# A float32 transpose of 8192 x 8192: store rows of 8 KB instead of 4 KB, pieces parked in shared slots and gathered by VectorE

## The chip, the cores and the metric

The kernel runs on one core of a Trainium2 chip. The metric is the device time of one launch in microseconds (us), as the median of several runs. Beside the runs there is one profiled execution, whose span goes from its first to its last instruction. Engines are called by their names or as the profile has them: PE (TensorE, its weight loads PEld), ACT (ScalarE), DVE (VectorE), POOL (GpSimd), SP (SyncE). Transfers between HBM and the on-chip memory (SBUF) run on 16 DMA engines, which take them from queues; the queue of ScalarE is q10 in the profile, that of SyncE q1.

## The reference

```python
def setup_inputs():
    return {"x": np.random.randn(8192, 8192).astype(np.float32)}

def reference(x):
    return np.transpose(x)
```

There is no arithmetic: 268 MB are read and 268 MB are written, with rows and columns exchanged.

## The kernel before

**Tiles.** The input is cut into chunks of 128 rows by 4096 columns, 2 MB each. Two bands of 4096 columns with 64 chunks each make 128 chunks, numbered t. A chunk is loaded into one of three input buffers (`ins`, `NIN = 3`), 16 KB in each of the 128 partitions. A *range* is a group of neighbouring columns of a band, which become rows of the output. Before the change a range has 512 columns (`B = 4` columns in each partition), and a band has 8 ranges.

**A chunk's way.** TensorE transposes the chunk with an identity matrix in 32 blocks of 128 x 128 (L117) into two PSUM tensors, one for each half of the ranges. It counts `s_pe` up as it goes. ScalarE copies the first half to SBUF and VectorE the second (both L241). A chunk gives each range one *piece*.

**Windows and stores.** The pieces of one range from 8 consecutive chunks (`W = 8`) lie side by side in one of 9 store buffers (`regs`, `NREG = 9`). Together they are a *window*: 2 MB, 16 KB in each partition, that is 4 output rows of 8 x 128 elements, 4 KB each. `wide_dma` (L28) describes a store so that the 16 KB of a partition are one packet with 4 rows at its far end. The ranges are staggered, so that exactly one window closes with each chunk. At the start, at the end, and where the second band begins, windows are shorter or come in two parts.

**The order.** Nothing is planned by a framework; the instructions are written out, and semaphores order them. The first three loads are issued by SyncE, all other loads (L103) and all stores (L28, the first L174) by ScalarE between its copies. In the steady part (`later(t)`) a store of a window that closed in chunk t is issued once the first transposes of chunk t+1 are done (`nc.scalar.wait_ge(s_pe, (t + 1) * NH + 1)`), and behind it the load of chunk t+3. TensorE starts a chunk when its load has landed and both copying engines are done with the chunk before (18 counts on `s_ld`). A copy that opens a window waits until the store that used its buffer has landed (`fresh`).

Of the kernel before, what the change touches and what calls it, by code (L numbers as in the profile page):

```python
# [40 lines left out]
def kernel(  # L41
# [22 lines left out]
    NR = S // B  # L64
    NIN = 3
    NREG = 9
    CH = N // P
    J = S * P

    with tc.tile_critical():  # L70
        nc.alloc_sbuf_tensor("pad", [P, 32], dt)
        ident = nc.alloc_sbuf_tensor("ident", [P, P], dt).ap()
        ins = [nc.alloc_sbuf_tensor(f"in{k}", [P, J], dt).ap() for k in range(NIN)]
        SIZE = B * W * P
        regs = nc.alloc_sbuf_tensor("regs", [P, NREG * SIZE], dt).ap()
        NH = NR // 2
        pss = [nc.alloc_psum_tensor(f"ps{k}", [P, NH * B * P], dt).ap() for k in range(2)]
# [3 lines left out]
        s_st = [nc.alloc_semaphore(f"s_st{k}") for k in range(NREG)]  # L81
        s_pe = nc.alloc_semaphore("s_pe")
        s_cp = [nc.alloc_semaphore("s_cpa"), nc.alloc_semaphore("s_cpv")]

# [3 lines left out]
            out=ident,  # L88
            in_=ident,
# [6 lines left out]
        nc.vector.sem_inc(s_ld[0], 1)  # L96
        nc.scalar.sem_inc(s_ld[0], 1)

        chunks = [(s, c) for s in range(M // J) for c in range(CH)]

        def load(t):
            s, c = chunks[t]
            (nc.sync if t < NIN else nc.scalar).dma_start(  # L103
                out=ins[t % NIN], in_=x[c * P:(c + 1) * P, s * J:(s + 1) * J]
            ).then_inc(s_ld[t % NIN], 16)

        def transposes(k):
            nc.tensor.sem_inc(s_ld[k], -18).wait_op(s_ld[k], 18, "sem-ge")  # L113
            for q in range(NR):
                e, g = divmod(q, NH)
                for b in range(B):
                    tr = nc.tensor.transpose(  # L117
                        pss[e][:, (g * B + b) * P:(g * B + b + 1) * P],
                        ins[k][:, q * B * P + b:(q + 1) * B * P - B + b + 1:B],
                        ident,  # L120
                    )
                if q % 2:
                    tr.then_inc(s_pe, 1)

        T = len(chunks)
        assert T % NIN == NIN - 1
        pe = [nc.tensor.engine]
        nc.tensor.wait_ge(s_id, 2)

# [13 lines left out]
        for t in range(NIN):  # L143
            load(t)

        copied = [0, 0]
        free = list(range(NREG))
        stored = [0] * NREG
        window = {}

        def later(t):
            return W <= t < T - NIN

        def store(q, e, t):
            t0, r, parts = window.pop(q)
            if later(t):
                nc.scalar.wait_ge(s_pe, (t + 1) * NH + 1)
            else:
                nc.scalar.wait_ge(s_cp[e], copied[e])
            base = 0  # L160
            pieces = []
            for s, a, z in parts:
                rows = (z - a) * P
                j0 = s * J + q * B * P
                dst = out[j0:j0 + B * P, a * P:a * P + rows]
                dst = dst.rearrange("(q b) i -> q b i", q=P)
                src = regs[:, r * SIZE + base:r * SIZE + base + B * rows]
                base += B * rows
                pieces.append((rows, dst, src))
            for rows, dst, src in sorted(pieces, key=lambda v: -v[0]):  # L170
                if any(stored):
                    st = wide_dma(nc, nc.scalar, "qActDynamicHW", dst, src)
                else:
                    st = nc.scalar.dma_start(  # L174
                        out=dst, in_=src.rearrange("q (b i) -> q b i", b=B)
                    )
                st.then_inc(s_st[r], 16)
                stored[r] += 1
            free.append(r)

        def closes(w, t):
            t0, r, parts = w
            return t + 1 == t0 + sum(z - a for _, a, z in parts)

        for t, (s, c) in enumerate(chunks):
            closed = []
            for e in range(2):
                eng = (nc.scalar, nc.vector)[e]
                go = s_ld[(t + 1) % NIN]

                place = []
                fresh = {}
                for q in range(e * NH, (e + 1) * NH):
                    if q not in window:

                        span = (q - c) % W + 1
                        r = free.pop(0)
                        parts = [(s, c, min(c + span, CH))]  # L200
                        if c + span > CH and t + span < T:
                            parts.append((s + 1, 0, c + span - CH))
                        window[q] = (t, r, parts)
                        if stored[r]:
                            fresh[q - e * NH] = (s_st[r], 16 * stored[r])
                    t0, r, parts = window[q]
                    k = [p[0] for p in parts].index(s)
                    base = r * SIZE + B * P * sum(z - a for _, a, z in parts[:k])
                    _, a, z = parts[k]
                    place.append((base + (c - a) * P, (z - a) * P))  # L210

                runs = []
                for g in range(NH):
                    if runs:
                        u = runs[-1]
                        gap = place[g][0] - place[g - 1][0]
                        if place[g][1] == place[u[0]][1] and abs(gap) < 2 ** 15 and (
                            len(u) == 1 or gap == place[u[1]][0] - place[u[0]][0]
                        ):
                            u.append(g)  # L220
                            continue
                    runs.append([g])
                if later(t):
                    runs = sorted(runs, key=lambda u: any(g in fresh for g in u))
                seen = t * NH + e * NH // 2
                for u in runs:
                    off, dist = place[u[0]]
                    gap = place[u[-1]][0] - place[u[-2]][0] if len(u) > 1 else 0
                    dims = [list(regs.ap[0]), [gap, len(u)], [dist, B], [1, P]]
                    o = bass.AP(regs.tensor, regs.offset + off, dims)  # L230
                    i = pss[e][:, u[0] * B * P:(u[-1] + 1) * B * P]
                    i = i.rearrange("p (l b i) -> p l b i", b=B, i=P)
                    need = t * NH + (e * NH + u[-1]) // 2 + 1
                    if later(t) and u is runs[0] and len(runs) > 1 and any(g in fresh for g in runs[-1]):
                        need = t * NH + (e * NH + max(v[-1] for v in runs)) // 2 + 1
                    if need > seen:
                        eng.wait_ge(s_pe, need)
                        seen = need
                    for sem, value in [fresh[g] for g in u if g in fresh]:
                        eng.wait_ge(sem, value)  # L240
                    cp = nc.scalar.copy(out=o, in_=i) if e == 0 else nc.vector.tensor_copy(out=o, in_=i)  # L241
                    ends = [e * NH + g for g in u if closes(window[e * NH + g], t)]
                    if later(t):
                        if u is runs[-1]:
                            cp.then_inc(go, 1)
                        closed += [(q, e) for q in ends]
                        continue
                    if ends:
                        cp.then_inc(s_cp[e], 1)
                        copied[e] += 1  # L250
                    if u is runs[-1]:
                        if ends:
                            eng.wait_ge(s_cp[e], copied[e])
                            eng.sem_inc(go, 1)
                        else:
                            cp.then_inc(go, 1)
                    for q in ends:
                        store(q, e, t)
            for q, e in closed:
                store(q, e, t)  # L260
            if t + NIN < T:
                if not closed:
                    nc.scalar.wait_ge(s_pe, (t + 1) * NH)
                load(t + NIN)
        for r in range(NREG):
            nc.sync.wait_ge(s_st[r], 16 * stored[r])
# [30 lines left out]
```

## Time and profile before

| what | us |
|---|---|
| median of 3 runs | 1262.53 (1261.64 to 1262.58) |
| span of the profiled execution | 1260.4 |
| VectorE busy in it | 302.0 |
| ScalarE busy in it | 253.5 |
| TensorE busy in it | 739.0 |

The page gives no other time for the profiled execution than its span; it is 2.1 us below the median of the runs, which also hold what lies around the first and the last instruction.

How to read the lines shown below. In a group of instructions stand line, engine, operation, output and input with their shapes, the count, then the busy time and the mean ns of one, then the idle time of the engine ahead of them and what ended it. In a timeline each line has start, duration, engine, line and operation, and in brackets the idle time before it; ACTq and SPq are DMA issues by ScalarE and SyncE. In windows each line is a stretch of the span with its length, then the busy time of each engine with its instructions (x), and last the granted clock of TensorE, the DMA share (busy share of the 16 engines, which can read 1.01 where packets overlap) and GB/s. In DMA issues the last number is the median time from the issue to the landing. Busy shares are averages over the span; what bounds a stretch is read from that stretch.

### The profile page before, as it was taken

How to read it: one execution, taken by the hardware profiler on the slowest of the kernel's cores; microseconds unless marked ns; L12 is line 12 of the kernel's file. 1: busy time of each engine (PE TensorE's matmuls, PEld its weight loads, DVE VectorE, ACT ScalarE, POOL GpSimd, SP SyncE). 2: the span in 40 equal slices, each digit the busy share in tenths (PEclk: the TensorE clock that was granted, in tenths of full speed). 3: DMA queues.
4: the chain of work that ended last, by engine and by line, in shares of the span. 5: the costliest groups of instructions: out<-in, count | busy, mean ns of one | idle time of the engine just before them, and what ended most of it. 6: DMA issues, size and time to landing. Idle time of an engine off the chain costs nothing. (4 is left out here: it accounts for less than half of the span.)

```text
span 1260.4 us, 9367 instructions
## 1 busy us (share of the span) xinstructions
PE 739.0 (59%) x4096; PEld 718.4 (57%) x4096; DVE 302.0 (24%) x250; ACT 253.5 (20%) x257; POOL 0.7 (0%) x6
## 2 busy tenths in 40 slices
PE   5656556565566655565556656566565655665561
PEld 5556556565556655565555656565565655665561
DVE  2322222222222222222222222222222222222220
ACT  3212211122111211122111211121111211121110
POOL 0000000000000000000000000000000000000000
PEclk9886876868777777778687786867777687777776
DMA  9999999999999999999999999999999999999998
GB/s 383 429 422 426 425 430 431 426 431 431 427 430 431 428 428 431 428 429 432 427 422 426 429 429 425 431 429 428 430 428 428 431 428 429 429 429 429 429 431 376
DMA packets 39271, 536.95 MB, mean 426 GB/s; under 512 B 4320, under 2 KB 4832, under 8 KB 6240
## 3 DMA queue, kind: packets, MB, share of 16 engines
q10 hardware_dynamic: 38832, 530.60, 99.0%
q1 hardware_dynamic: 432, 6.29, 1.2%
q14 instruction: 6, 0.05, 0.0%
q8 instruction: 1, 0.02, 0.0%
HBM read 268.44 MB, written 268.44 MB: 426 GB/s over the span
## 5 line engine op out<-in xcount | busy, mean ns | idle before, releaser
L117 PE MATMUL ps<-ident,in 128*128 128x128 f32 x4096 | 739.0, 362 | 493.5 <-PEq L113 493.5
L117 PEld LDWEIGHTS ps<-ident,in 128*128 128x128 f32 x4096 | 718.4, 220 | 513.9 <-issue 513.9
L241 DVE COPY regs<-ps 128x512 f32<-128x512 f32 (+3 forms) x250 | 302.0, 1246 | 932.1 <-PE ps L117 932.1
L241 ACT COPY regs<-ps 128x512 f32<-128x512 f32 (+3 forms) x256 | 252.2, 1016 | 978.8 <-PE ps L117 760.8
L241 ACT ACT_TABLE_LOAD x1 | 1.3, 1283 | 1.0 <-SPq L70 1.0
L87 POOL TENSOR_SCALAR_AFFINE_SELECT ident<-ident 128x128 f32<-128x128 f32 x1 | 0.3, 293 | 0.2 <-POOL ident L85 0.2
L85 POOL MEMSET ident<- 128x128 f32 x1 | 0.2, 204 | 0.5 <-SPq L70 0.5
L281 POOL MEMSET const-bfloat16-1.0<- 128x1 bf16 x1 | 0.1, 102 | 0.0
L281 POOL MEMSET const-uint8-127<- 128x1 uint8 x1 | 0.1, 102 | 0.0
L281 POOL MEMSET const-float32-0.0<- 128x1 f32 x1 | 0.1, 99 | 0.2 <-issue 0.2
L281 POOL MEMSET const-float32-1.0<- 128x1 f32 x1 | 0.1, 99 | 0.0
## 6 DMA issues: line engine op xcount, KB each, us to landing
in<-in_x_dram ACTq DMA_DIRECT2D x125, 2048.0 KB, 16.8
out_dram<-regs ACTq DMA_DIRECT2D x114, 2048.0 KB, 12.6
out_dram<-regs ACTq DMA_DIRECT2D x4, 1792.0 KB, 11.1
in<-in_x_dram SPq DMA_DIRECT2D x3, 2048.0 KB, 11.7
out_dram<-regs ACTq DMA_DIRECT2D x4, 1536.0 KB, 12.5
out_dram<-regs ACTq DMA_DIRECT2D x4, 1280.0 KB, 11.5
out_dram<-regs ACTq DMA_DIRECT2D x4, 1024.0 KB, 11.1
out_dram<-regs ACTq DMA_DIRECT2D x4, 768.0 KB, 12.3
```

What stands on the lines that cost most here:

```text
L85: nc.gpsimd.memset(ident, 0.0).then_inc(s_id, 1)
L87: nc.gpsimd.affine_select(out=ident, in_=ident, compare_op=mybir.AluOpType.not_equal, fill=1.0, base=0, pattern=[[-1, P]], channel_multipl ...
L117: tr = nc.tensor.transpose(pss[e][:, (g * B + b) * P:(g * B + b + 1) * P], ins[k][:, q * B * P + b:(q + 1) * B * P - B + b + 1:B], ident,)
L241: cp = nc.scalar.copy(out=o, in_=i) if e == 0 else nc.vector.tensor_copy(out=o, in_=i)
L281: nc = _bacc.Bacc("TRN2", target_bir_lowering=False, num_devices=1)
```

## The change

A range now has 256 columns (`B = 2`), so a band has 16 ranges (`NR = 16`), and a window collects 16 chunks. A full window is still 2 MB with 16 KB in each partition, now as 2 output rows of 8 KB.

Sixteen open windows of 2 MB don't fit in SBUF. So a piece isn't put where it will be stored from. It waits in a *slot*. The slot of range r and chunk t is found from the pair of r and m = t mod 16, and the pair (r, m) shares its slot with (m, r): 120 slots of 128 KB each. Window w (range w mod 16) closes with chunk w. Before the copies of chunk w VectorE gathers the window's earlier pieces, up to 15, from their slots into a place in the `arena` (`gather`), and counts `s_g` up. The last piece is copied from PSUM straight to that place by ScalarE or VectorE, ahead of the other pieces of its quarter, and counts `s_cl` up. Both engines' copies of chunk t wait for `s_g` to reach t, since they write into slots which that gather empties.

The arena holds the three input buffers and 38 pieces more. A loop at build time gives each window a place in it (`home`) and notes whose store must have landed before (`before`); near the end the places may lie in input buffers, and the gather then waits for the transposes of the buffer's last chunk.

TensorE waits for each half of PSUM by itself (`s_free`) and signals after each quarter of a chunk instead of each pair of ranges. All loads and stores are issued by SyncE: `store(t)` waits for `s_cl`, and behind it come the loads. Up to chunk 15 and from chunk 124 on, loads are issued up to chunk t+3, between them up to t+2. After the last chunk 15 short windows are gathered and stored. The gathers of windows 127 and 128 are begun a chunk early, ahead of the copies of chunks 126 and 127.

```diff
-    S = 32
-    B = 4
-    W = 8
+    B = 2
+    NR = 16
+    W = NR
+    J = NR * B * P
     NIN = 3
-    NREG = 9
+    PIECE = B * P
+    FIN = 38
+    NQ = 4
+    QR = NR // NQ
...
+        slots = nc.alloc_sbuf_tensor("slots", [P, (NR * (NR - 1) // 2) * PIECE], dt).ap()
+        arena = nc.alloc_sbuf_tensor("arena", [P, NIN * J + FIN * PIECE], dt).ap()
...
         def transposes(k):
-            nc.tensor.sem_inc(s_ld[k], -18).wait_op(s_ld[k], 18, "sem-ge")
+            for h in range(2):
+                nc.tensor.sem_inc(s_free[h], -1).wait_op(s_free[h], 1, "sem-ge")
+                if h == 0:
+                    nc.tensor.sem_inc(s_ld[k], -16).wait_op(s_ld[k], 16, "sem-ge")
...
+                    if g % QR == QR - 1:
+                        tr.then_inc(s_pe, 1)
...
+        def slot(r, t):
+            m = t % W
+            d = (r - m) % W
+            if d < W // 2:
+                return ((d - 1) * W + m) * PIECE
+            if d > W // 2:
+                return ((W - d - 1) * W + r) * PIECE
+            return ((d - 1) * W + min(r, m)) * PIECE
...
+        def gather(w, upto):
+            from_ = begun.get(w, max(0, w - W + 1))
+            begun[w] = upto
+            for u in before.pop(w, []):
+                if isinstance(u, tuple):
+                    nc.vector.wait_ge(s_pe, (u[1] + 1) * NQ)
+                else:
+                    nc.vector.wait_ge(s_st[u % W], done[u])
...
+            if r < NR // 2 and runs:
+                nc.vector.wait_ge(s_cp[0], upto)
+            for v in runs:
+                so, do, dist = v[0]
+                ss, ds = (v[1][0] - so, v[1][1] - do) if len(v) > 1 else (PIECE, P)
+                cp = nc.vector.tensor_copy(
+                    out=ap(arena, do, [[ds, len(v)], [dist, B], [1, P]]),
+                    in_=ap(slots, so, [[ss, len(v)], [P, B], [1, P]]),
+                )
+            if runs and upto == min(w, T):
+                cp.then_inc(s_g, 1)
...
+        def copies(t):
+            for e, eng in enumerate((nc.scalar, nc.vector)):
+                if t:
+                    eng.wait_ge(s_g, t)
+                for h in range(NQ // 2):
+                    eng.wait_ge(s_pe, t * NQ + e * NQ // 2 + h + 1)
...
+                    runs.sort(key=lambda v: (v[0][1] is not None))
...
+        def store(w):
+            if w < T:
+                nc.sync.wait_ge(s_cl, w + 1)
             else:
-                nc.scalar.wait_ge(s_cp[e], copied[e])
+                nc.sync.wait_ge(s_g, w)
...
+        EARLY = W
+        LATE = T - NIN - 1
+        loaded = NIN
+        for t in range(T):
+            gather(t, t)
+            if t >= T - 2:
+                gather(t + 1, t)
+            copies(t)
+            store(t)
+            upto = t + NIN if t < EARLY or t >= LATE else t + NIN - 1
+            while loaded <= min(upto, T - 1):
+                nc.sync.wait_ge(s_pe, (loaded - NIN + 1) * NQ)
+                load(loaded)
+                loaded += 1
+        for w in range(T, T + W - 1):
+            gather(w, T)
+            store(w)
```

More of the change, by code (lines that the diff above doesn't have):

```diff
@@ L141, with parts @@
         nc.switch_bb("done")
[L143 to L157, printed above, removed]
-            else:
-                nc.scalar.wait_ge(s_cp[e], copied[e])
-            base = 0
+        def parts(w):
+            first, last = max(0, w - W + 1), min(w, T - 1)
+            cut = [first] + [t for t in range(first + 1, last + 1) if t % CH == 0] + [last + 1]
+            return list(zip(cut[:-1], cut[1:]))
@@ new lines, in cells @@
+        def cells(w):
+            return sum(z - a for a, z in parts(w))
+        def slot(r, t):
[6 more added lines that the diff above has]
+            return ((d - 1) * W + min(r, m)) * PIECE
+        users = []
+        home = {}
+        before = {}
+        end = NIN * NR + FIN
+        for w in range(T + W - 1):
+            n = cells(w)
+            best = None
+            low = NIN * NR if w < T - 2 else 0
+            for o in range(low, end - n + 1):
+                over = [(u, when) for u, a, z, when in users if a < o + n and o < z]
+                cost = max([when for _, when in over], default=-1)
+                for k in range(NIN):
+                    if o < (k + 1) * NR and k * NR < o + n:
+                        t = [t for t in range(T) if t % NIN == k][-1]
+                        over.append((("in", t), t + 1))
+                        cost = max(cost, t + 1)
+                if best is None or cost < best[0]:
+                    best = (cost, o, [u for u, _ in over])
+            home[w], before[w] = best[1], best[2]
+            users = [v for v in users if not (v[1] < best[1] + n and best[1] < v[2])]
+            users.append((w, best[1], best[1] + n, w + 3))
@@ new lines, in place, with ap @@
+        def place(w, t):
+            base = home[w] * PIECE
+            for a, z in parts(w):
+                if a <= t < z:
+                    return base + (t - a) * P, (z - a) * P
+                base += (z - a) * PIECE
+        stored = [0] * W
+        done = {}
+        def ap(tensor, off, dims):
+            return bass.AP(tensor.tensor, tensor.offset + off, [list(tensor.ap[0])] + dims)
+        begun = {}
+        def gather(w, upto):
[6 more added lines that the diff above has]
+                    nc.vector.wait_ge(s_st[u % W], done[u])
+            r = w % NR
+            runs = []
+            for t in range(from_, upto):
+                so, (do, dist) = slot(r, t), place(w, t)
+                if runs:
+                    v = runs[-1]
+                    step = (so - v[-1][0], do - v[-1][1])
+                    if dist == v[0][2] and do > v[-1][1] and (
+                        len(v) == 1 or step == (v[1][0] - v[0][0], v[1][1] - v[0][1])
+                    ) and (len(v) > 1 or step[1] == P):
+                        v.append((so, do, dist))
+                        continue
+                runs.append([(so, do, dist)])
+            if r < NR // 2 and runs:
[6 more added lines that the diff above has]
+                    in_=ap(slots, so, [[ss, len(v)], [P, B], [1, P]]),
+                )
+            if runs and upto == min(w, T):
+                cp.then_inc(s_g, 1)
@@ L161, in store @@
+        def store(w):
+            if w < T:
+                nc.sync.wait_ge(s_cl, w + 1)
+            else:
+                nc.sync.wait_ge(s_g, w)
+            s_w = s_st[w % W]
             pieces = []
-            for s, a, z in parts:
+            base = home[w] * PIECE
+            r = w % NR
+            for a, z in parts(w):
+                s, c = divmod(a, CH)
                 rows = (z - a) * P
-                j0 = s * J + q * B * P
-                dst = out[j0:j0 + B * P, a * P:a * P + rows]
+                j0 = s * J + r * PIECE
+                dst = out[j0:j0 + PIECE, c * P:c * P + rows]
@@ L166, in store @@
                 dst = dst.rearrange("(q b) i -> q b i", q=P)
[L167 removed]
+                pieces.append((rows, dst, arena[:, base:base + B * rows]))
                 base += B * rows
[L169 removed]
             for rows, dst, src in sorted(pieces, key=lambda v: -v[0]):
[L171 to L176 removed]
@@ L177, in store @@
[L177 to L264, printed above, removed]
@@ L265 @@
-        for r in range(NREG):
-            nc.sync.wait_ge(s_st[r], 16 * stored[r])
+                if w:
+                    st = wide_dma(nc, nc.sync, "qSPDynamicHW", dst, src)
+                else:
+                    st = nc.sync.dma_start(out=dst, in_=src.rearrange("q (b i) -> q b i", b=B))
+                st.then_inc(s_w, 16)
+                stored[w % W] += 16
+            done[w] = stored[w % W]
+        EARLY = W
[12 more added lines that the diff above has]
+                loaded += 1
@@ L270 @@
+        for w in range(T, T + W - 1):
+            gather(w, T)
+            store(w)
+        for k in range(W):
+            nc.sync.wait_ge(s_st[k], stored[k])
 _INS = ['x']
```

81 lines of the change are left out of this document (52 added, 29 removed).

## The prediction

> **What bounds the kernel now.** I read the page from its top: the engine shares, the slices, the queues.
>
> ```profile
> span 1260.4 us, 9367 instructions
> PE 739.0 (59%) x4096; PEld 718.4 (57%) x4096; DVE 302.0 (24%) x250; ACT 253.5 (20%) x257; POOL 0.7 (0%) x6
> DMA  9999999999999999999999999999999999999998
> DMA packets 39271, 536.95 MB, mean 426 GB/s; under 512 B 4320, under 2 KB 4832, under 8 KB 6240
> q10 hardware_dynamic: 38832, 530.60, 99.0%
> ```
>
> No compute engine is busy for more than 59% of the span; the sixteen DMA engines are busy in every slice, and one queue, ScalarE's (q10), takes 99% of their time. The bytes are fixed: 268 MB in, 268 MB out. So only three things can move the time: what a transfer costs the DMA engines beside its bytes, stretches in which they have nothing to do, and the two ends. The stretches of the span, by windows (last column GB/s, before it the DMA share):
>
> ```profile
> 20.00:150.00 130.00, 79.22 (x480) 76.80 (x480) 36.80 (x36) 30.16 (x33) 0.00 (x0) 0.82 1.01 424
> 190.00:600.00 410.00, 246.06 (x1344) 239.29 (x1344) 99.04 (x79) 81.59 (x75) 0.00 (x0) 0.75 1.01 429
> 610.00:700.00 90.00, 53.11 (x292) 51.69 (x293) 21.98 (x30) 17.51 (x18) 0.00 (x0) 0.75 1.01 425
> 700.00:1200.00 500.00, 300.92 (x1641) 292.69 (x1640) 119.11 (x80) 99.96 (x94) 0.00 (x0) 0.75 1.01 429
> ```
>
> The steady rate is 429. It falls to 425 where the band changes (610 to 700) and to 424 in the first stretch, both with the DMA engines full: there the stores are cut into smaller packets. One steady chunk in the timeline:
>
> ```profile
> 347.24 6.58 PE L117 MATMUL ps<-ident,in 128*128 128x128 f32 x32 [3.38 <-PEq L113]
> 349.23 0.55 ACTq L28 DMA_DIRECT2D out_dram<-regs  x1
> 349.81 0.61 ACTq L103 DMA_DIRECT2D in<-in_x_dram  x1
> ...
> 353.85 2.36 DVE L241 COPY regs<-ps 128x1024 f32<-128x1024 f32 x2 [7.66 <-PE ps L117]
> 357.01 5.31 PE L117 MATMUL ps<-ident,in 128*128 128x128 f32 x32 [3.19 <-PEq L113]
> ...
> 366.76 5.51 PE L117 MATMUL ps<-ident,in 128*128 128x128 f32 x32 [4.44 <-PEq L113]
> ```
>
> A chunk comes every 9.76 us ((366.76 - 347.24) / 2): one load and one store of 2 MB, 4.88 us each, 0.305 us for each piece of 128 KB. VectorE starts 0.03 us after the modelled end of the transposes (353.82). How much work is queued ahead is in the issues:
>
> ```profile
> in<-in_x_dram ACTq DMA_DIRECT2D x125, 2048.0 KB, 16.8
> out_dram<-regs ACTq DMA_DIRECT2D x114, 2048.0 KB, 12.6
> ```
>
> A load lands 16.8 us after its issue and needs 4.88, so the queue is 12 us deep. That depth is what the change spends.
>
> **The change, part by part.** I write s12 for the store of window 12, l15 for the load of chunk 15.
>
> *Packets and rows.* A full store stays 2 MB in 128 packets of 16 KB, now 2 rows of 8 KB instead of 4 of 4 KB. Stores before: 114 full and 28 partial (7 sizes, four of each). After: windows 0 to 14 and 128 to 142 are short and windows 64 to 78 come in two parts, so 60 partial and 98 full. No row prices a row of a packet. The nearest is the band change: 7 stores in two parts are 896 more packets, and (429 - 425) / 429 of 90 us is 0.84 us, times 16 engines 13.4 us, so 15 ns for a packet with its 4 rows. Per engine (8 packets a store) there are 128 more packets; the rows fall from 142 x 8 x 4 = 4544 to 158 x 8 x 2 = 2528. If all 15 ns are the packet: +1.9 us. If all are rows (3.75 ns each): -7.6 us. The two ends rest on the same row, so I halve it (7.5 and 1.9 ns): +1.0 - 3.8 = **-2.8 us**.
>
> *The queue.* Loads and stores all move from ScalarE's queue to SyncE's, in the order s(t), l(t+2) from chunk 17 on, and s(t), l(t+3) before. ScalarE loses two issues a chunk; its idle time costs nothing. SyncE waits for the closing copy of window t, and l(t+2) stands behind that wait. When chunk t has landed the queue holds s(t-1) and l(t+1): 9.76 us. In that time s(t) must arrive, and the tightest case is a window whose piece is in the last quarter (t mod 16 of 12 to 15, on VectorE). Its rows, with the start of the first load:
>
> ```profile
> 0.94 1.32 SPq L103 DMA_DIRECT2D in<-in_x_dram  x3
> ...
> 8.40 5.50 PE L117 MATMUL ps<-ident,in 128*128 128x128 f32 x32 [8.40 <-PEq L113]
> ```
>
> ```profile
> 0.00:2.20 2.20, 0.00 (x0) 0.00 (x0) 0.00 (x0) 1.22 (x1) 0.70 (x6) 1.00 0.15 30
> 2.20:2.70 0.50, 0.00 (x0) 0.00 (x0) 0.00 (x0) 0.06 (x1) 0.00 (x0) 1.00 0.98 262
> 2.70:3.20 0.50, 0.00 (x0) 0.00 (x0) 0.00 (x0) 0.00 (x0) 0.00 (x0) 1.00 0.46 164
> 3.20:3.70 0.50, 0.00 (x0) 0.00 (x0) 0.00 (x0) 0.00 (x0) 0.00 (x0) 1.00 1.15 492
> ```
>
> ```profile
> L241 DVE COPY regs<-ps 128x2048 f32<-128x2048 f32 x45 | 103.1, 2292 | 334.3 <-PE ps L117 334.3
> L241 DVE COPY regs<-ps 128x1024 f32<-128x1024 f32 x77 | 91.1, 1219 | 269.0 <-PE ps L117 269.0
> L241 DVE COPY regs<-ps 128x512 f32<-128x512 f32 x103 | 66.1, 685 | 282.3 <-PE ps L117 282.3
> L241 ACT COPY regs<-ps 128x1024 f32<-128x1024 f32 x72 | 72.1, 1013 | 248.5 <-PE ps L117 178.1 <-issue 61.6 <-DMA out_dram<-regs 7.5
> ```
>
> Issued at 0.94, the first load's packets start between 2.2 and 3.2, so 1.3 to 2.2 us from issue to data, 1.75 taken. The VectorE rows give 1.04 ns an element and 0.15 us an instruction: 0.42 us for a piece of 256. Two semaphore hops I allow 0.1 us each (an estimate; the 0.03 above is the nearest row). Then 5.3 to 6.58 (transposes) + 0.42 + 0.2 + 1.3 to 2.2 = 7.2 to 9.4 us, below 9.76. So no gap in the steady part, by 0.4 us at worst; other quarters have 1.4 us or more besides. Price **0**; what it costs without that margin is the first rival.
>
> *The gather.* VectorE takes on 15 pieces (3840 elements, two or three instructions) for each window, between copies(t-1) and copies(t), and ScalarE's copies wait for it. No row copies out of SBUF. Upper end: the PSUM rate, 3840 x 1.04 + 0.3 = 4.3 us; lower end: the instructions' fixed part alone, 0.3. No row is near, so I take the middle, 2.3. VectorE then has 2.3 + 4 x 1.22 / 2 = 4.8 us of 9.76 (6.8 at the upper end). The loop gather, ScalarE's copies (2 x 1.01), next transposes (6.58), VectorE's last quarter (1.4) is 12.3 us for two chunks of 19.5: hidden. Its buffer: window w's place in the 38-piece arena is w-2's, and s(w-2) ends before l(w) begins, 4.88 us before the chunk lands: hidden too.
>
> *The head.* By the placement loop two windows get the place of the one before them: 13 (over 11 and 12) and 15 (over 13 and 14). The queue there is l14, s12, l15, s13: gather 13 waits for s12 to land, when only l15 is left, 4.88 us. The chain is gather of 13 pieces (0.3 to 3.8; 2.0), a quarter 1.22, closing piece 0.42, hops 0.2, 1.75 to data: 5.6, a gap of 0.7. Window 15 the same with 2.3: 5.9, gap 1.0. Together **+1.7 us** (0 to 5.5).
>
> *The tail.* At chunk 126 the early gather of window 127 stands ahead of copies(126) on VectorE and waits, for its place in the input buffer, until the transposes of 126 are done.
>
> ```profile
> 1227.04 5.45 PE L117 MATMUL ps<-ident,in 128*128 128x128 f32 x32 [4.51 <-PEq L113]
> ...
> 1233.38 15.33 ACTq L28 DMA_DIRECT2D out_dram<-regs  x5
> ```
>
> So s126 comes 5.45 + 2.2 (14 pieces, 0.3 to 4.0) + 1.22 + 0.42 + 0.2 + 1.75 = 11.2 us after chunk 126 starts; the queue lasts 9.76: gap 1.5. Transposes of 127's second half wait for copies(126), but VectorE is later: 9.3 (closing piece) + 1.1 (rest) + 0.42 + 2.2 (window 128's gather) + 1.22 + 0.42 + 0.2 + 1.75 = 16.6 against 11.2 + 4.88: gap 0.5. Together **+2.0 us** (0 to 5.6). Behind it each gather (at most 4.3 us, less with each window) is shorter than the store before it, and the stores queue as the last five do now (15.33 us of issue).
>
> *Engines apart.* The DMA engines finish at different times now:
>
> ```profile
> 1256.00:1257.00 1.00, 0.00 (x0) 0.00 (x0) 0.00 (x0) 0.00 (x0) 0.00 (x0) 0.50 0.77 328
> 1257.00:1258.00 1.00, 0.00 (x0) 0.00 (x0) 0.00 (x0) 0.00 (x0) 0.00 (x0) 0.50 0.31 131
> 1258.00:1259.00 1.00, 0.00 (x0) 0.00 (x0) 0.00 (x0) 0.00 (x0) 0.00 (x0) 0.50 0.04 16
> ```
>
> Up to 3 us lie between them. With a queue 12 us deep that lead does no harm; with a shallow one a leading engine runs dry and its lead is lost. 0 to 2.6; I take **+1.0**.
>
> Sum: 1260.4 - 2.8 + 0 + 1.7 + 2.0 + 1.0 = 1262.3. The median of the runs, 1262.5, stands 2.1 above the profiled span, so the forecast is **1264.4**, +0.15%. A measurement tells about 0.2% (2.5 us) from no change: 1260.0 to 1265.1 counts as the same.
>
> **The rivals.**
> 1. *The store comes late in every cycle* (slower). If issue to data, the clock or a hop takes the last quarter past 9.76 us by b, the queue runs dry; one late store shifts the next landing, so every second of 4 such chunks pays: 8 cycles x 2 x b = 16 b. It decides from 0.4 us beyond my longest case. For it: one cold start is all that prices issue to data. Against: 5.3 to 5.5 us transposes leave over 1 us. With b = 0.5: 1272.
> 2. *Rows pay and the gaps vanish* (faster). Near the lower end of the gather both ends are without gaps; with rows between half and all: 1260.4 - 5 + 2.1 = 1257.5. For it: the margin of 0.5 to 1.5 us in each gap is small.
> 3. *The gather runs at the PSUM rate*: gaps 11.1 instead of 3.7, 1271.8. For it: the only VectorE rows there are. The Trainium skill (VectorE: DVE Perf Modes, section Mode 2×_2P) says that a copy with one source, both sides in SBUF, moves two fp32 elements a cycle. No row here shows it; by it the gather would be half the upper end and this rival would fall.
> 4. *The longer rows do nothing*: +1.9 instead of -2.8, 1269. For it: the packet stays 16 KB. [...]
>
> **How the numbers follow.** Forecast 0.33, rivals 0.16, 0.26, 0.14, 0.11. The forecast's own range is 1261 to 1267, mostly inside the same band. Faster is rival 2 with a little of it in the same band; slower is rivals 1, 3 and 4 with an edge of the forecast. The range runs from rival 2's full price (1257) to rival 1 at b of 0.8 (1276).
>
> **What would show it.** Right: 9.76 us between chunks, 429 GB/s in the steady windows with the share at 1.0, gathers of 2.3 us, short dips of the share near 100 us and in the last 60, DMA share full otherwise. Wrong: a dip once in every 16 chunks (rival 1); over 430 in the steady windows and no dips (rival 2); gathers of 4 us (rival 3); 429 with dips only at the ends, yet the band change slower than now (rival 4).

## The result and the profile after

The changed kernel takes 1318.4 us where the one before takes 1262.6: a ratio of 1.045, 95% interval 1.042 to 1.048. The forecast was 1264.4, its range 1257 to 1276. The profiled execution has a span of 1316.8 us, 56.4 more than before. In three of the kernels below one execution of four was over 1.5% slower than the others (in the one with the store at the second quarter it is the profiled one), and their medians leave it out. First the page of the kernel after: engine shares, packets, the one queue, and two groups of DMA issues (last column: us from issue to landing).

```profile
span 1316.8 us, 10808 instructions
PE 723.0 (55%) x4096; PEld 702.5 (53%) x4096; DVE 615.6 (47%) x718; ACT 267.8 (20%) x401; POOL 0.7 (0%) x6
DMA packets 41328, 537.03 MB, mean 408 GB/s; under 512 B 4576, under 2 KB 5216, under 8 KB 8288
q1 hardware_dynamic: 41312, 536.89, 99.4%
arena<-in_x_dram SPq DMA_DIRECT2D x128, 2048.0 KB, 14.9
out_dram<-arena SPq DMA_DIRECT2D x98, 2048.0 KB, 10.3
```

VectorE's busy time doubled and is still only 47% of the span; TensorE's went down a little. No compute engine became the bound. The bytes are the same, the mean rate fell from 426 to 408. Loads land 14.9 us after their issue instead of 16.8, stores 10.3 instead of 12.6: the queue is about 2 us shallower. Now the same stretches as before, by windows (last two columns: DMA share, GB/s):

```profile
20.00:150.00 130.00, 79.17 (x525) 76.82 (x525) 63.36 (x77) 32.26 (x50) 0.00 (x0) 0.82 0.98 401
190.00:600.00 410.00, 238.48 (x1280) 232.03 (x1280) 192.61 (x220) 83.65 (x123) 0.00 (x0) 0.72 1.00 411
610.00:700.00 90.00, 54.45 (x288) 53.00 (x288) 41.06 (x48) 19.03 (x31) 0.00 (x0) 0.72 1.01 407
700.00:1200.00 500.00, 278.16 (x1561) 270.45 (x1562) 233.97 (x273) 102.36 (x152) 0.00 (x0) 0.78 1.00 411
```

This says where the 56 us are. With the rates of before (424, 429, 425, 429): 130 x 23 / 424 = 7.1 us in the first stretch, 410 x 18 / 429 = 17.2, 90 x 18 / 425 = 3.8 and 500 x 18 / 429 = 21.0 in the later ones, and the remaining 7 us nearly all after 1200 us. So 42 of 56 us are lost in the steady part, which the prediction had priced at -2.8 for the rows, 0 for the queue and 1.0 for the engines apart.

The trap is the share, the column ahead of the rate: it reads 1.00 while the rate is 4% down. In this trace a packet that takes longer is recorded as a longer packet (1208 ns instead of 611 in the slow places), so engines that move less still look full. The rate shows the loss, the share does not.

A steady piece of the timeline, chunks whose closing piece lies in the last quarter:

```profile
404.83 6.34 PE L114 MATMUL ps<-ident,arena 128*128 128x128 f32 x32 [3.83 <-PEq L110]
...
410.30 0.42 DVE L253 COPY arena<-ps 128x256 f32<-128x256 f32 x1 [5.14 <-PE ps L114]
410.64 2.08 DVE L253 COPY slots<-ps 128x768 f32<-128x768 f32 x2
410.75 0.55 SPq L28 DMA_DIRECT2D out_dram<-arena  x1
411.34 0.59 SPq L85 DMA_DIRECT2D arena<-in_x_dram  x1
412.86 2.35 DVE L218 COPY arena<-slots 128x1792 f32<-128x1792 f32 x2
416.01 5.75 PEld L114 LDWEIGHTS ps<-ident,arena 128*128 128x128 f32 x32 [5.03 <-issue]
416.04 5.91 PE L114 MATMUL ps<-ident,arena 128*128 128x128 f32 x32 [4.87 <-PEq L110]
...
422.68 0.55 SPq L28 DMA_DIRECT2D out_dram<-arena  x1
```

The store is issued 5.9 us after its chunk starts (410.75 - 404.83). With the 1.3 to 2.2 us from issue to data of the prediction it arrives at 7.2 to 8.1, inside the 7.2 to 9.4 that was forecast and well inside 9.76. (The store of the next chunk, shown last, is issued 6.6 us after its chunk's start.) And still the next chunk starts 11.21 us later instead of 9.76. The gather (412.86, 2.35 us) is over 0.8 us before the transposes start, and holds nothing up. By quarters of the closing piece, first to last, the store is issued 2.4, 4.0, 5.4 and 6.4 us after its chunk's start (means of the trace). All periods became longer, not only those of the last quarter: worked out from the starts of chunks 18 to 123, grouped by t mod 16,

```
t mod 16     0      1      2      3      4      5      6      7
us       11.38  10.16  10.68  10.00   9.88  10.17  10.09  10.14
t mod 16     8      9     10     11     12     13     14     15
us       10.03  10.26  10.25  10.29  10.02  10.53  10.23  10.58
```

(before: 9.76 to 9.80 in every row). The longest is the one after the last chunk of a cycle.

The ends, by windows of the kernel after: the head gaps of windows 13 and 15 with the stretches behind them, and the tail gap of window 126.

```profile
105.00:112.00 7.00, 0.32 (x2) 0.35 (x3) 4.59 (x7) 1.99 (x3) 0.00 (x0) 0.50 0.74 316
112.00:118.00 6.00, 6.00 (x35) 6.00 (x34) 3.08 (x3) 2.09 (x3) 0.00 (x0) 0.62 1.04 380
118.00:124.00 6.00, 3.84 (x31) 3.57 (x30) 1.48 (x4) 0.00 (x0) 0.00 (x0) 1.00 0.98 350
124.00:134.00 10.00, 0.25 (x1) 0.28 (x2) 4.78 (x6) 1.99 (x3) 0.00 (x0) 0.64 0.85 362
134.00:140.00 6.00, 6.00 (x40) 6.00 (x40) 3.98 (x5) 1.99 (x3) 0.00 (x0) 0.74 1.06 374
140.00:147.00 7.00, 3.47 (x29) 3.30 (x28) 5.50 (x7) 2.05 (x4) 0.00 (x0) 1.00 0.97 365
147.00:162.00 15.00, 5.76 (x35) 5.59 (x34) 7.27 (x9) 2.05 (x4) 0.00 (x0) 0.62 1.01 425
...
1265.00:1270.00 5.00, 2.63 (x20) 2.28 (x19) 4.86 (x8) 1.99 (x3) 0.00 (x0) 1.00 0.65 275
```

The gaps are there: 0.26 x 7 = 1.8 us for window 13 (forecast 0.7), 0.15 x 10 = 1.5 for window 15 (forecast 1.0), 0.35 x 5 = 1.75 for 126 and 127 (forecast 2.0). But the stretches behind each head gap run at 350 to 380 with the share near 1, which the sum did not have: that is the other half of the 7 us lost at the head.

### The profile page after: what moved, and what is told of

It is laid out like the page before. It is cut to its first block, busy times and chain, and to the rows that moved or that the text cites. A ratio compares the mean times of both kernels' runs of the same rounds, so it can differ in the third digit from the quotient of the medians.

```text
span 1316.8 us, 10808 instructions
## 1 busy us (share of the span) xinstructions
PE 723.0 (55%) x4096; PEld 702.5 (53%) x4096; DVE 615.6 (47%) x718; ACT 267.8 (20%) x401; POOL 0.7 (0%) x6
## 5 line engine op out<-in xcount | busy, mean ns | idle before, releaser
L114 PE MATMUL ps<-ident,arena 128*128 128x128 f32 x4096 | 723.0, 357 | 546.5 <-PEq L110 544.7
L114 PEld LDWEIGHTS ps<-ident,arena 128*128 128x128 f32 x4096 | 702.5, 218 | 566.7 <-issue 566.6
L253 DVE COPY slots<-ps 128x512 f32<-128x512 f32 (+2 forms) x336 | 292.2, 912 | 451.8 <-PE ps L114 451.6
L253 ACT COPY slots<-ps 128x1024 f32<-128x1024 f32 (+2 forms) x336 | 249.7, 773 | 754.9 <-PE ps L114 697.5
L218 DVE COPY arena<-slots 128x2048 f32<-128x2048 f32 (+7 forms) x318 | 304.5, 1007 | 70.3 <-DMA out_dram<-arena 42.4
L253 DVE COPY arena<-ps 128x256 f32<-128x256 f32 x64 | 26.9, 420 | 155.1 <-PE ps L114 155.0
L253 ACT COPY arena<-ps 128x256 f32<-128x256 f32 x64 | 23.9, 373 | 245.9 <-PE ps L114 221.0
## 6 DMA issues: line engine op xcount, KB each, us to landing
arena<-in_x_dram SPq DMA_DIRECT2D x128, 2048.0 KB, 14.9
out_dram<-arena SPq DMA_DIRECT2D x98, 2048.0 KB, 10.3
out_dram<-arena SPq DMA_DIRECT2D x4, 1920.0 KB, 10.3
out_dram<-arena SPq DMA_DIRECT2D x4, 1408.0 KB, 12.2
```

Of the source, the lines that this page charges most:

```text
L114: tr = nc.tensor.transpose(pss[h][:, (g * B + b) * P:(g * B + b + 1) * P], ins[k][:, q * PIECE + b:(q + 1) * PIECE - B + b + 1:B], ident,)
L218: cp = nc.vector.tensor_copy(out=ap(arena, do, [[ds, len(v)], [dist, B], [1, P]]), in_=ap(slots, so, [[ss, len(v)], [P, B], [1, P]]),)
L253: cp = eng.copy(out=dst, in_=i) if e == 0 else eng.tensor_copy(out=dst, in_=i)
```

## The experiments

The theories, as they stood after the result. *Rows*: stores with rows of 8 KB are slower. *Queue*: SyncE's queue is slower than ScalarE's. *Gather*: VectorE's copies inside the on-chip memory take bandwidth from the DMAs. *Depth*: the store (and the load behind it) is issued too late, although it reaches the queue before the queue is empty.

**Rows, in the kernel before.** Only the shape of the destination block is changed. By the condition in the code this holds for 84 of the 114 full stores (7 of 8 ranges, 6 windows each, 2 bands), not for the 96 that the expectation names:

```diff
+ k = (a - q - 1) // W
+ if z - a == W and len(parts) == 1 and q < W - 1 and k < CH // W - 2:
+     j1, a1 = j0 + k % 2 * 2 * P, a - k % 2 * W
+     dst = out[j1:j1 + 2 * P, a1 * P:a1 * P + 2 * rows]
+     dst = dst.rearrange("(q b) i -> q b i", q=P)
```

> The kernel before, with nothing changed but where 96 of its 114 full stores put their rows: 2 rows of 8 KB instead of 4 of 4 KB, so blocks of the output are exchanged. Rows theory (long rows are what costs 56 us): about 1262 + 96/98 of 50, over 1300. Depth theory (the store and the load behind it reach the queue too late; the rows are innocent): 1258 to 1263, a little faster if the rows saved what the prediction took for them (2.8 us).

Measured: 1259.46 us against 1261.99 in the same session, ratio 0.9989 (0.9974 to 1.0004). The windows (190 to 600, the steady rate):

```profile
190.00:600.00 410.00, 247.86 (x1347) 241.11 (x1348) 99.08 (x79) 81.69 (x75) 0.00 (x0) 0.74 1.01 431
```

431 instead of 429 (at 700 to 1200 this execution, of 1266.9 us, falls to 425). The medians differ by 2.5 us, but the interval still holds no change. Longer rows certainly cost nothing.

**Rows, in the kernel after.** Full stores go as 4 rows of 4 KB into another DRAM tensor:

```diff
+ other = nc.dram_tensor("other", (M, N), dt, kind="Internal").ap()
...
+ if rows == W * P:
+     dst = other[r * 4 * P:(r + 1) * 4 * P, w // NR * 8 * P:(w // NR + 1) * 8 * P]
```

> The changed kernel, its full stores written as 4 rows of 4 KB into another DRAM tensor, so the full windows are missing from the output; bytes, packets, queue and gather stay. Rows theory: back to about 1265. Depth theory: stays at 1318 or a few us above (1316 to 1326).

Measured: 1321.69, ratio 1.047 (1.0453 to 1.0488), steady rates 408 and 411. The loss stays whatever the rows: the rows theory falls.

**Queue.** The kernel before with every load and store issued by SyncE at the same points:

```diff
- (nc.sync if t < NIN else nc.scalar).dma_start(
+ nc.sync.dma_start(
...
- nc.scalar.wait_ge(s_pe, (t + 1) * NH + 1)
+ nc.sync.wait_ge(s_pe, (t + 1) * NH + 1)
...
- st = wide_dma(nc, nc.scalar, "qActDynamicHW", dst, src)
+ st = wide_dma(nc, nc.sync, "qSPDynamicHW", dst, src)
```

> The kernel before with all loads and stores issued by SyncE instead of ScalarE, at the same points (store t after the first quarter of the transposes of chunk t+1). Queue theory (SyncE's queue is slower): over 1290. Depth theory: 1260 to 1265, since the store comes as early as before.

Measured: 1262.18, ratio 1.0003 (0.9994 to 1.0013). SyncE's queue costs nothing. Its steady window:

```profile
190.00:600.00 410.00, 250.40 (x1344) 243.61 (x1344) 99.00 (x79) 81.84 (x75) 0.00 (x0) 0.73 1.01 429
```

**Depth.** The same kernel, with the store (and the load behind it on the queue) waiting for the second, third or last quarter of the chunk's transposes instead of the first. The data stored has been ready all along; nothing else is changed.

```diff
- nc.sync.wait_ge(s_pe, (t + 1) * NH + 1)
+ nc.sync.wait_ge(s_pe, (t + 1) * NH + 2)    # and + 3, + 4
```

> The kernel before on SyncE's queue, each store waiting for the second quarter of the transposes: issued some 3.4 us after the chunk starts (2.0 gave 1262, 6.2 gave 1333). Depth theory: a threshold between; with 6.4 us left of the 9.8 queued I expect the same as 2.0 or up to 1270.

> The same with the third quarter: issued some 4.8 us after the chunk starts, 5 us left. Depth theory: between, 1275 to 1310.

> As the run before this one, but each store, and with it the load behind, waits for the last quarter of the transposes, so it is issued some 6 us after the chunk starts instead of 2, as late as the changed kernel's last-quarter windows. Rows of 4 KB, no gather. Depth theory: 1290 to 1330, with short slow stretches at the end of loads and stores although the queue is never empty. Rows and VectorE theories: unchanged, 1260 to 1266.

Measured:

```
store issued after chunk start     2.0     3.7    5.3    5.5 us
time                               1262.2  1297.9 1316.3 1332.8 us
ratio                              1.0003  1.0269 1.0418 1.0561
95% interval, from                 0.9994  1.0230 1.0389 1.0544
              to                   1.0013  1.0308 1.0446 1.0579
```

The first line has the medians of the traces; the expectations took 3.4, 4.8 and 6.2 from the schedule. The last two lie close together: TensorE's granted clock at 190 to 600 us was 0.67 in the trace of the one and 0.80 in that of the other, so that its quarters are shorter there. A quarter of the last kernel's stores come 5.9 us or more after the start, but the median issue alone does not explain the 16.5 us between these two. The last two kernels came out above the ranges expected, 1275 to 1310 and 1290 to 1330. The windows and the two issue groups of the last of these, the store at the last quarter:

```profile
190.00:600.00 410.00, 220.75 (x1263) 214.30 (x1263) 94.03 (x71) 76.56 (x65) 0.00 (x0) 0.80 1.00 406
700.00:1200.00 500.00, 277.52 (x1538) 269.80 (x1539) 113.16 (x76) 94.65 (x85) 0.00 (x0) 0.77 1.00 406
...
in<-in_x_dram SPq DMA_DIRECT2D x128, 2048.0 KB, 14.3
out_dram<-regs SPq DMA_DIRECT2D x114, 2048.0 KB, 9.5
```

and two chunks of its timeline:

```profile
400.88 5.39 PE L117 MATMUL ps<-ident,in 128*128 128x128 f32 x32 [3.14 <-PEq L113]
...
406.30 0.55 SPq L28 DMA_DIRECT2D out_dram<-regs  x1
...
406.89 0.59 SPq L103 DMA_DIRECT2D in<-in_x_dram  x1
412.28 6.37 PE L117 MATMUL ps<-ident,in 128*128 128x128 f32 x32 [6.01 <-PEq L113]
```

This is the kernel before, without a gather, with its rows of 4 KB, and it shows all the marks of the changed one: share 1.00 at 406 GB/s, landings after 14.3 and 9.5 us, 11.4 us between two chunks although the store is issued 5.4 us after the first starts. One thing moved, the time at which the store and the load behind it are issued. The expectation of a threshold falls too: already the second quarter costs 36 us, and every later one costs more.

**Depth, given back in the kernel after.** The load is queued one chunk further ahead all the way, as in the first 16 chunks; everything else (gather, long rows, SyncE) stays. A second version has one more place in the input and piece arena.

```diff
- EARLY = W
+ EARLY = T
```

```diff
- FIN = 38
+ FIN = 39
```

> The changed kernel with loads issued three chunks ahead throughout (EARLY = T instead of W); rows, gather, arena and queue stay. A chunk that has landed then has up to 19.5 us of transfers behind it instead of 9.8, though a gather now waits for the store of window w-2 to land 4.9 us after its chunk. Depth theory: the steady rate returns to 429 or a little over, and 1318 falls to 1260 to 1272 (the gaps at the head stay). If VectorE's copies in SBUF hold up the transfers: stays over 1300.

> As a_early, with 39 pieces of arena instead of 38: window 13 then waits for no store, 14 for 11 and 12, and only window 16 still waits for the store just before it (15). If the two waits at windows 13 and 15 cost what the profile shows (DMA share down to 0.74 and 0.85 in the head), 2 to 6 us under a_early; if the queue's depth hides them, the same.

Measured: 1313.59, ratio 1.0396 (1.0361 to 1.0431), and 1308.85, ratio 1.0355 (1.0326 to 1.0384). As a total the first misses: I expected nearly all of it back. The second is 4.7 us under it, inside the 2 to 6 expected, but the two intervals overlap. The windows of the first one show why:

```profile
190.00:600.00 410.00, 244.28 (x1328) 237.50 (x1327) 201.66 (x230) 83.77 (x129) 0.00 (x0) 0.74 1.01 430
610.00:700.00 90.00, 54.15 (x294) 52.70 (x294) 43.16 (x51) 18.10 (x30) 0.00 (x0) 0.75 1.01 429
700.00:1200.00 500.00, 282.56 (x1531) 274.78 (x1529) 228.49 (x266) 94.17 (x148) 0.00 (x0) 0.74 0.99 403
...
750.00:800.00 50.00, 28.51 (x165) 27.70 (x164) 23.90 (x27) 10.08 (x17) 0.00 (x0) 0.77 1.01 431
900.00:1000.00 100.00, 58.62 (x310) 56.98 (x309) 45.26 (x53) 18.17 (x31) 0.00 (x0) 0.72 1.00 401
1000.00:1100.00 100.00, 51.69 (x288) 50.24 (x288) 43.22 (x49) 17.78 (x25) 0.00 (x0) 0.76 0.96 379
```

Up to 800 us the changed kernel, with every gather and every 8-KB row, runs at 430 (431 at 750 to 800). So the gather theory falls, and the steady loss of the change goes away with a deeper queue alone. Then the rate breaks. In this version the gather waits for the store of two windows earlier, as VectorE's waits say (us in total, times, longest):

```profile
DVE arena L218 <- DMA out_dram<-arena: 615.6, 115, 13.3
```

That store counts as done when the slowest of the 16 DMA engines ends it. From 461 us on one engine runs 1.5% slower than the rest (a chunk each 9.87 us instead of 9.73), and the distance from first to last engine grows from 3.6 to 9.9 us at 892 (and to 14.4 at 1238). The next work is released by the slowest engine and eaten first by the fastest: at 887 the leaders have used up the whole queue, and from there up to 1200 a chunk takes 9.9 to 11.5 us, most of them over 10.6. This is read from the packets of the trace; why one engine lags was not tested.

**Depth, by an earlier closing copy.** TensorE's loop is written out, and each chunk begins with the quarter of the closing range, so that the last-quarter stores go out as early as the others. Again also with the larger arena.

```diff
+ def order(t):
+     c = t % NR // QR
+     return [c, c ^ 1, c ^ 2, c ^ 3]
...
+ for n, c in enumerate(order(t)):
...
- s_cl = nc.alloc_semaphore("s_cl")
+ s_cl = [nc.alloc_semaphore("s_cla"), nc.alloc_semaphore("s_clv")]
```

> The changed kernel, its result and its 38 pieces kept, but TensorE (its loop written out) begins each chunk with the quarter that holds the closing range, and both copying engines take the quarters in that order. Every store is then issued some 2.2 us after its chunk starts, not 2.2 to 6. If the lead of the store over the engine that needs it first is what costs: 427 to 431 GB/s in the steady windows, some 43 us less than the changed kernel, about 1270 to 1280 with the gaps at head and tail left in. If gather or arena cost it: 1310 to 1320.

> As a_rot, with 39 pieces of arena: one wait for the store just before instead of two at the head (window 16 for 15). Lead theory: 2 to 5 us under a_rot.

Measured: 1289.46, ratio 1.0193 (1.0139 to 1.0247), and 1289.81, ratio 1.022 (1.0197 to 1.0243). The first one's windows and issues:

```profile
190.00:600.00 410.00, 246.04 (x1341) 239.44 (x1342) 203.06 (x230) 84.37 (x127) 0.00 (x0) 0.74 1.01 427
700.00:1200.00 500.00, 288.98 (x1593) 280.91 (x1592) 241.30 (x279) 102.60 (x156) 0.00 (x0) 0.75 1.01 419
...
arena<-in_x_dram SPq DMA_DIRECT2D x128, 2048.0 KB, 16.6
out_dram<-arena SPq DMA_DIRECT2D x98, 2048.0 KB, 12.2
```

Work, rows, gather and queue order are those of the changed kernel; only the order of the quarters (with TensorE's loop written out for it) is not, and 29 of the 56 us come back. The median time of the store's issue is now 2.45 us after the chunk's start. The landings return to nearly those of before (16.6, 12.2). I had expected 1270 to 1280; the later windows (418, 419) do not reach 429. The larger arena cures the head (419 instead of 405 at 20 to 150) and gains nothing in total where 2 to 5 us were expected, since 190 to 600 falls to 422.

**Depth, both ways, by the wait alone.** In one kernel the closing copy is left out for windows 16 to 124 and their stores wait for the gather only; in the other every store waits for all copies of its chunk.

```diff
+ if o is None and W <= t < T - NIN:
+     continue
...
- if w < T:
+ if w < W or T - NIN <= w < T:
...
```

```diff
- nc.sync.wait_ge(s_cl, w + 1)
+ nc.sync.wait_ge(s_cp[0], w + 1)
+ nc.sync.wait_ge(s_cp[1], w + 1)
```

> The changed kernel without the copy of the closing piece for windows 16 to 124 (one of 16 pieces of each is left out, so the output lacks them); their stores wait for the gather alone and are issued about when the chunk lands. Lead theory: as a_rot or a little less, 1265 to 1280. Gather theory: still over 1305.

> The changed kernel with each store waiting until both engines have copied the whole chunk, so every window is issued as late as a last-quarter one or later, 7 to 8 us after the chunk starts. Lead theory: the loss that the late quarters have now in all of them, 1340 to 1380. If the lead is not the cause: 1316 to 1322.

Measured: 1280.67, ratio 1.0159 (1.0124 to 1.0193), a little over the 1265 to 1280 expected, and 1327.06, ratio 1.0518 (1.0501 to 1.0536). The windows of the one with early stores:

```profile
20.00:150.00 130.00, 74.96 (x526) 72.61 (x525) 63.73 (x77) 31.72 (x48) 0.00 (x0) 0.86 0.98 400
190.00:600.00 410.00, 244.16 (x1332) 237.58 (x1333) 191.29 (x204) 82.29 (x110) 0.00 (x0) 0.74 1.01 430
700.00:1200.00 500.00, 296.08 (x1614) 287.84 (x1613) 236.94 (x259) 98.18 (x132) 0.00 (x0) 0.75 1.01 424
```

The steady rate is 430 with every gather running. What is left lies in the head (400, as in the changed kernel), in the later stretch (424; its engines are 7 us apart) and in the tail. With all stores late the steady rates are 409 and 408 and the time grows by only 9 us; I expected 22 to 62. Most of what lateness can cost here is paid already when a part of the stores is late.

**What a short lead costs.** From the packets of the traces: the lead of a store is the time from its issue to the moment when the leading DMA engine ends the transfer ahead of it; beside it what the store's transfer takes beyond 4.87 us, averaged over the 16 engines and the stores (their number in brackets).

```
lead                    0 to 1 us     1 to 2 us    2 to 3 us    over 3 us
kernel after            +1.21 (8)     +0.41 (29)   +0.05 (12)   about 0
after, 4-KB rows        +1.22         +0.29        +0.05
before, 3rd quarter                   +0.37
before, last quarter                  +0.41
after, all stores late                +0.45 (56)
after, quarters turned                +0.18 (14)   +0.04 (45)
before                                             +0.02 to 0.03
```

A few stores came when the leading engine had already run dry: one in the kernel after (+1.9), four in the one with 4-KB rows (+2.1 on average). The same order stands in kernels with and without gather, with either row length: a store needs about 2 to 3 us of lead over the leading engine. The price is not one number: at 1 to 2 us of lead it is +0.29 to +0.45 where the engines are 3 us apart or less, and +0.18 with the quarters turned, where they are 4.7 apart. In the slow transfers all leading engines are in step, and the last one or two packets of each take up to 1208 ns instead of 611.

The table does not hold the whole loss. By the same count the stores of the kernel after lose 0.35 us a chunk in the steady stretches and the loads 0.14, and no load has a short lead (5.7 us at the least). Up to 600 us the loads lose 0.01 in the version with loads three chunks ahead and in the one without the closing copy, which run at 430 there; what slows them in the kernel after was not tested.

## Why the prediction was wrong

**The step that failed is "The queue ... Price 0".** Its chain to the store was right: transposes, closing copy, hops and start add up to 7.2 to 8.1 us for the first store shown and to at most 8.9 for the second (issued 6.7 us after its chunk's first weight load), inside the forecast 7.2 to 9.4. The room was wrong. I set it to 9.76 us, the work queued when a chunk has landed. But a chunk starts 0.47 us after the slowest of the 16 engines has landed its part, and the leading engine is ahead by then. Three stores, worked out from the packets (us; a chunk starts with its first weight load, and the first and the last engine end the transfer ahead of the store at the times given):

```
kernel   chunk starts   store issued   first engine   last engine   lead
before      396.02         398.03         401.82         405.30     3.8
after       404.80         410.75         412.47         415.53     1.7
after       416.01         422.68         422.43         425.26    -0.3
```

In the kernel before the room is 401.82 - 396.02 = 5.8 us, which is 9.76 - 3.47 (first to last engine) - 0.47, and not 9.76. The prediction noted up to 3 us between the engines at the end of the run, and put it into a term of its own instead of taking it off the margin. The stores of the last quarter, issued 6.4 us after their chunk's start on average, have 1.3 us of lead on average (2.6 to -0.3), where the table asks for 2 to 3, somewhat more than the 1.3 to 2.2 of a cold start. The third row shows what follows: the first engine runs dry, and behind that transfer the engines are 0.85 us apart instead of 2.8.

**"Engines apart", +1.0 with an upper end of 2.6, had the right mechanism as a one-time loss.** It repeats. In the trace after (times of landing), the engines are 0.5 us apart at 161 and 2.3 at 250, and fall back to 0.5 to 0.9 at a store that comes too late, again and again. Why every row of the table of periods is longer, and not only those for the last quarter, the packets tell in part. Stores of the third quarter are late too: they have 1.4 us of lead on average, and a store with the load ahead of it takes 0.6 us too long there, 0.8 in the last quarter. In the first two quarters it is 0.3, for the first quarter all of it in the loads, whose cause is open.

**Rival 1** named the direction, a store that comes late in every cycle, with the wrong point (past 9.76 us) and price (16 b: the steady loss of 42 us would need a b of 2.6; by the same 16 b the range's end of 1276 is a b of 0.7, not 0.8). It confined the loss to 4 of 16 chunks; the runs show it spread over all.

**Rows, -2.8: right in sign.** The kernel before with long rows is 2.5 us faster by its medians, at 431 instead of 429, though its interval just includes no change. By the steady transfers of these two traces (an eighth of a transfer's time on an engine, medians) a packet of 16 KB takes 608 ns in a load, 612 in a store of four rows and 608 in one of two rows: so there is a cost on the row, some 2 ns, close to the 1.9 that the sum took. Rival 4 falls with that. The Trainium skill (DMA: Bandwidth & Descriptors, section Why small descriptors are slow) names a fixed overhead of about 3 cycles per packet, and 32 bytes of metadata for each DMA operation that joining descriptors into packets does not save. The 4 ns inside a packet do not come from the first, and no run here shows whether they come from the second.

**Gather, 2.3 us and hidden: right.** These are VectorE's groups by form of the kernel after (count, busy time, mean ns):

```profile
L218 DVE COPY arena<-slots 128x2048 f32<-128x2048 f32 x125 | 152.4, 1219 | 22.1 <-DVE slots L253 11.6 <-DMA out_dram<-arena 10.3
L218 DVE COPY arena<-slots 128x1792 f32<-128x1792 f32 x70 | 85.6, 1223 | 23.1 <-DMA out_dram<-arena 9.6 <-PE ps L114 6.3
L218 DVE COPY arena<-slots 128x1280 f32<-128x1280 f32 x26 | 24.8, 952 | 13.5 <-DMA out_dram<-arena 13.3
L218 DVE COPY arena<-slots 128x1536 f32<-128x1536 f32 x15 | 14.3, 954 | 0.4
...
L218 DVE COPY arena<-slots 128x1024 f32<-128x1024 f32 x20 | 13.7, 683 | 4.5 <-DMA out_dram<-arena 4.2
```

A whole gather takes 2.35 us. (1219 - 683) / 1024 is 0.52 ns an element, half of the 1.04 out of PSUM: rival 3 falls. The Trainium skill, which it set against itself (VectorE: DVE Perf Modes, section Mode 2×_2P), has two fp32 elements a cycle for such a copy, and the trace agrees.

**SyncE's queue at nothing: right** (1262.18 against 1261.99).

**Head +1.7 and tail +2.0: right in place, too small.** The gaps measure 3.3 and 1.75 us. But the head loses 7, since the stretches behind a gap run at 350 to 380; I priced a gap as its length alone. Behind the gaps the engines are in step (0.5 us apart at 161); that the leads lost in the gap are what slows these stretches is likely, but no run tests it. At the tail I compare when each kernel has moved the same number of bytes: the kernel after is behind by 50.1 us at 1200, by 53.8 at 1250 and by 57.0 at 1314. So 3.7 us are still lost in ordinary chunks, and the tail proper, from chunk 126 on (1257), costs some 3 us against the forecast 2.0.

**What stays open.** That a store with a short lead has slow last packets was seen in the traces; why it has them was not tested, and neither was why the loads lose 0.14 us a chunk. Open too is why one engine runs 1.5% slower in long deep-queue stretches, which spoils the version with the deeper queue after 800 us. None of the runs gives a kernel with the reference's output that beats the one before.

## What to carry to other kernels

When transfers keep 16 DMA engines full, count the room for the next issue from the leading engine, not from the landing that starts the compute (the slowest one), and keep 2 to 3 us beyond that; here an issue 1.7 us later (3.7 instead of 2.0) cost 36 us in 1262, and one 3.5 us later 71. Read a bandwidth-bound stretch by its GB/s, since a DMA share of 1.00 stood over a loss of 4%. And a change that saves something in a transfer (here 2.5 us by rows) should first be charged for what it does to the depth of the queue.

## What the runs showed of the hardware

- A DMA that is issued late, though before its queue is empty, slows its own transfer of 4.87 us: in the kernel after +1.2 us at 0 to 1 us of lead, +0.4 at 1 to 2, nothing above 3.
- The 16 engines are 2 to 4 us apart in the kernel before and drift up to 14.4 us apart in the one with the deep queue; there one engine was 1.5% slower from 461 to 887 us.
- VectorE's copy inside the on-chip memory costs an odd number of 256-element pieces like the next even one: 1792 elements 1223 ns and 2048 elements 1219, 1280 elements 952 and 1536 elements 954.
- On a queue that had run dry, a store issued at 110.94 us (kernel after) moved its first packets on the 16 engines at 112.14 to 112.29: 1.2 to 1.35 us.
